# Storing a softmax tile two loads behind instead of three, with the last stores between the last exponentials

## The chip, the cores and the metric

One core of a Trainium2 chip runs the kernel. The metric is the device time of one execution in microseconds; a profiled execution also gives a span, about 1.8 us shorter. Executions of one kernel mostly agree within 0.3%. Differences below are a few microseconds of 1330, so most kernels were timed in five rounds, interleaved with the kernel before on the same chip.

## The reference

```python
# x: float32 [4, 4096, 4352], G = 8 groups of 544 columns in every row
x_g = x.reshape(B, N, G, Dg)
x_g = x_g - x_g.max(axis=-1, keepdims=True)
exp = np.exp(x_g)
out = exp / exp.sum(axis=-1, keepdims=True)
```

Each of the 16384 rows is read once and written once: 285.2 MB in, 285.2 MB out.

## The kernel before

A tile is 128 partitions x 2 rows, 4.46 MB; there are 64 tiles in 6 buffers, worked in place. The sync engine issues the loads, VectorE takes the maxima and scales, ScalarE takes the exponentials and issues the stores.

```python
R = 2; NT = 6; LAG = 3             # rows of a partition, buffers, tiles between load and store
# ... (cut: views, semaphores, take() waits for a semaphore and lowers it)

def vector_max(n):                 # row n: 1 reduction; at a tile's first row wait for its load, raise `seen`
def vector_scale(n):               # row n: wait for its exponentials, 1 reciprocal, 8 multiplications

def scalar_exp(n):
    take(nc.scalar, max_done)
    for g in range(G):
        i = nc.scalar.activation(...)          # exp(x - max), sums accumulated
    i.then_inc(exp_done, 1)

def store(b, target):
    take(nc.scalar, scaled, R)
    nc.scalar.dma_start(out=target, in_=bufs[b][:, :]).then_inc(stored[b], 16)

def scalar_tile(j, target=None):
    take(nc.scalar, seen)
    if target is not None:
        store((j - LAG) % NT, target)
    for r in range(R):
        scalar_exp(j * R + r)

for t in range(nt):                            # the loads' queue
    if t >= NT:
        nc.sync.wait_ge(stored[t % NT], 16 * (t // NT))
    nc.sync.dma_start(out=bufs[t % NT][:, :], in_=xt[t]).then_inc(landed[t % NT], 16)

for j in range(LAG):                           # ScalarE's program
    scalar_tile(j)
with loop(nc.scalar) as u:
    for b in range(NT):
        scalar_tile(LAG + b, turn_out[u, b])
for j in range(rest, nt):
    scalar_tile(j, ot[j - LAG])
for t in range(nt - LAG, nt):
    store(t % NT, ot[t])
# ... (cut: VectorE's program: maximum of row n+1, then scaling of row n; a loop of 12 rows)
```

Of the kernel before, what the change touches and what calls it, by code (L numbers as in the profile page):

```python
# [1 line left out]

# [5 lines left out]


@with_exitstack  # L10
def kernel(
    ctx: ExitStack,
    tc: tile.TileContext,
    x: bass.AP,
    out: bass.AP,
):
    nc = tc.nc
    G = 8
    P = 128
    R = 2  # L20
    NT = 6
    S = R * NT
    LAG = 3
    xf = x.flatten_outer_dims()
    of = out.flatten_outer_dims()
    N, D = xf.shape
    Dg = D // G
    nt = N // (P * R)
    turns = (nt - LAG) // NT
    rest = LAG + turns * NT  # L30
    f32 = mybir.dt.float32
    X = mybir.AxisListType.X
    Exp = mybir.ActivationFunctionType.Exp
    xt = xf.rearrange("(t p r) d -> t p (r d)", p=P, r=R)
    ot = of.rearrange("(t p r) d -> t p (r d)", p=P, r=R)
    turn_out = of[:turns * S * P, :].rearrange("(u b p r) d -> u b p (r d)", b=NT, p=P, r=R)

    landed = [tc.alloc_semaphore(f"landed{b}") for b in range(NT)]
    stored = [tc.alloc_semaphore(f"stored{b}") for b in range(NT)]
    seen = tc.alloc_semaphore("seen")  # L40
    max_done = tc.alloc_semaphore("max_done")
    exp_done = tc.alloc_semaphore("exp_done")
    rec_done = tc.alloc_semaphore("rec_done")
    scaled = tc.alloc_semaphore("scaled")

    ctx.enter_context(tc.tile_critical(no_gpsimd_drain=True))  # L46
    bufs = [ctx.enter_context(nc.sbuf_tensor(f"xt{b}", [P, R * D], f32)) for b in range(NT)]
    mx = ctx.enter_context(nc.sbuf_tensor("mx", [P, S, G], f32))
    sm = ctx.enter_context(nc.sbuf_tensor("sm", [P, S, G], f32))
    rs = ctx.enter_context(nc.sbuf_tensor("rs", [P, S, G], f32))  # L50

    def loop(engine):

        return nc.Fori(
            0, turns, engines=OrderedEngineSet([engine.engine]), head_slot={engine.engine: 0})

    def take(engine, sem, n=1):
        engine.sem_inc(sem, -n).wait_op(sem, n, "sem-ge")  # L58

    def row(s):  # L60
        b, r = divmod(s, R)
        return bufs[b][:, r * D:(r + 1) * D].rearrange("p (g d) -> p g d", g=G)

    def vector_max(n):
        s = n % S
        if s % R == 0:
            take(nc.vector, landed[s // R], 16)
            nc.vector.sem_inc(seen, 1)
        nc.vector.reduce_max(out=mx[:, s, :], in_=row(s), axis=X, negate=True).then_inc(max_done, 1)  # L69

    def vector_scale(n):
        s = n % S
        take(nc.vector, exp_done)
        nc.vector.reciprocal(out=rs[:, s, :], in_=sm[:, s, :]).then_inc(rec_done, 1)  # L74
        take(nc.vector, rec_done)
        xr = row(s)
        for g in range(G):
            i = nc.vector.tensor_scalar_mul(  # L78
                out=xr[:, g, :], in0=xr[:, g, :], scalar1=rs[:, s, g:g + 1])
        i.then_inc(scaled, 1)  # L80

    def scalar_exp(n):
        s = n % S
        take(nc.scalar, max_done)
        xr = row(s)
        for g in range(G):
            i = nc.scalar.activation(  # L87
                out=xr[:, g, :],
                in_=xr[:, g, :],
                func=Exp,  # L90
                bias=mx[:, s, g:g + 1],
                scale=1.0,
                accum_out=sm[:, s, g:g + 1],
            )
        i.then_inc(exp_done, 1)

    def store(b, target):
        take(nc.scalar, scaled, R)
        nc.scalar.dma_start(out=target, in_=bufs[b][:, :]).then_inc(stored[b], 16)

    def scalar_tile(j, target=None):

        take(nc.scalar, seen)
        if target is not None:
            store((j - LAG) % NT, target)
        for r in range(R):
            scalar_exp(j * R + r)


    for t in range(nt):  # L110
        b = t % NT
        if t >= NT:
            nc.sync.wait_ge(stored[b], 16 * (t // NT))
        nc.sync.dma_start(out=bufs[b][:, :], in_=xt[t]).then_inc(landed[b], 16)
    for b in range(NT):
        nc.sync.wait_ge(stored[b], 16 * ((nt - b + NT - 1) // NT))


    nc.scalar.preload_act_table(Exp)  # L119
    for j in range(LAG):  # L120
        scalar_tile(j)
    with loop(nc.scalar) as u:
        for b in range(NT):
            scalar_tile(LAG + b, turn_out[u, b])
    for j in range(rest, nt):
        scalar_tile(j, ot[j - LAG])
    for t in range(nt - LAG, nt):
        store(t % NT, ot[t])


    def vector_rows(lo, hi):
        for n in range(lo, hi):
            vector_max(n + 1)
            vector_scale(n)

    vector_max(0)
    vector_rows(0, LAG * R)
    with loop(nc.vector):
        vector_rows(LAG * R, LAG * R + S)
    vector_rows(rest * R, nt * R - 1)  # L140
    vector_scale(nt * R - 1)


# [1 line left out]
_INS = ['x']  # L145
_OUTS = [((4, 4096, 4352), 'float32')]


# [23 lines left out]
```

## Time and profile before

| | before |
|---|---|
| time, median of the first 3 runs | 1334.18 us |
| span of the profiled run | 1332.2 us |
| share of VectorE, ScalarE | 78%, 57% |
| load, store: median from issue to landing | 28.4, 33.2 us |
| steady rate of the transfers | 433 GB/s |

The first two numbers are the metric and what the profile accounts for. The shares say that no compute engine bounds the kernel; the steady rate says that the transfers do. The two medians show that each transfer spends most of its time queued: a tile alone needs 10.3 us of all 16 engines. The prediction shows the lines.

Two readings below go under the profile's tables, to the trace's record of every DMA packet. A packet is one partition's part of a tile, 34816 bytes in 1.288 us, on one of 16 DMA engines. The records don't name the engine, but an engine's next packet starts 3 ns before its last one ends, so packets can be joined end to end into chains, one for each engine. Near the end of a run the joins are plain; earlier, several engines often end within a few ns of one another, and a long chain is then one of several that fit. *Idleness* of a stretch is its length minus the packet time in it over 16, each packet counted 3 ns shorter for the overlap.

### The profile page before, as it was taken

The page shows a single profiled execution, that of the slowest core. Times are in us where ns is not written, and L with a number is a line of the kernel's source. Part 1 is how long each engine was busy: PE and PEld are TensorE (multiplying, and loading weights), DVE is VectorE, ACT ScalarE, POOL GpSimd, SP SyncE. Part 2 cuts the span into 40 slices and gives each one's busy share as a digit, 9 for nine tenths or more (in the row PEclk, how much of TensorE's full clock was granted, in tenths as well). Part 3 has the DMA queues.
Part 4 walks back from the last instruction along what each step waited for, and adds up shares of the span by engine and source line. Part 5 has one row for each costly group of instructions (what it writes and reads, how often), then busy time and mean ns, then how long its engine had stood idle before and what let it go on. Part 6 is the DMA issues. An engine that isn't in the chain of part 4 may idle for free. (4 is left out here: it accounts for less than half of the span.)

```text
span 1332.2 us, 4328 instructions
## 1 busy us (share of the span) xinstructions
DVE 1041.5 (78%) x1280; ACT 764.4 (57%) x2049; POOL 0.2 (0%) x4
## 2 busy tenths in 40 slices
DVE  5999887877878778778787787877878778778781
ACT  3777655655556555565565655655556555565560
POOL 0000000000000000000000000000000000000000
DMA  9999999999999999999999999999999999999988
GB/s 401 417 400 425 433 431 433 434 433 433 433 432 433 435 435 434 432 433 435 432 433 433 433 433 435 434 434 433 433 434 432 434 433 432 433 435 435 434 373 386
DMA packets 18439, 570.49 MB, mean 428 GB/s; under 512 B 2048, under 2 KB 2048, under 8 KB 2048
## 3 DMA queue, kind: packets, MB, share of 16 engines
q1 hardware_dynamic: 9216, 285.22, 49.7%
q10 hardware_dynamic: 9216, 285.22, 49.7%
q14 instruction: 7, 0.06, 0.0%
HBM read 285.21 MB, written 285.21 MB: 428 GB/s over the span
## 5 line engine op out<-in xcount | busy, mean ns | idle before, releaser
L87 ACT ACTIVATE xt<-xt,mx 128x544 f32<-128x544 f32 x1024 | 751.2, 734 | 536.7 <-ACTq L58 536.7
L69 DVE TENSOR_REDUCE mx<-xt 128x8 f32<-128x4352 f32 x128 | 599.0, 4680 | 240.9 <-DVEq L58 240.9
L78 DVE TENSOR_SCALAR xt<-xt,rs 128x544 f32<-128x544 f32 x1024 | 434.0, 497 | 19.2 <-DVEq L58 0.9
L87 ACT ACTIVATION_READ_ACCUMULATOR xt<-xt,mx 128x1 f32 x1024 | 191.1, 187 | 0.0
L74 DVE RECIPROCAL rs<-sm 128x8 f32<-128x8 f32 x128 | 24.5, 191 | 4.2 <-DVEq L58 4.2
L119 ACT ACT_TABLE_LOAD x1 | 1.3, 1283 | 0.9 <-SPq L46 0.9
L156 POOL MEMSET const-bfloat16-1.0<- 128x1 bf16 x1 | 0.1, 103 | 0.0
L156 POOL MEMSET const-uint8-127<- 128x1 uint8 x1 | 0.1, 102 | 0.0
L156 POOL MEMSET const-float32-0.0<- 128x1 f32 x1 | 0.1, 100 | 0.2 <-issue 0.2
L156 POOL MEMSET const-float32-1.0<- 128x1 f32 x1 | 0.1, 99 | 0.0
## 6 DMA issues: line engine op xcount, KB each, us to landing
xt<-in_x_dram SPq DMA_DIRECT2D x64, 4352.0 KB, 28.4
out_dram<-xt ACTq DMA_DIRECT2D x64, 4352.0 KB, 33.2
```

The lines of the kernel that those rows point to most:

```text
L69: nc.vector.reduce_max(out=mx[:, s, :], in_=row(s), axis=X, negate=True).then_inc(max_done, 1)
L74: nc.vector.reciprocal(out=rs[:, s, :], in_=sm[:, s, :]).then_inc(rec_done, 1)
L78: i = nc.vector.tensor_scalar_mul(out=xr[:, g, :], in0=xr[:, g, :], scalar1=rs[:, s, g:g + 1])
L87: i = nc.scalar.activation(out=xr[:, g, :], in_=xr[:, g, :], func=Exp, bias=mx[:, s, g:g + 1], scale=1.0, accum_out=sm[:, s, g:g + 1],)
L119: nc.scalar.preload_act_table(Exp)
L156: nc = _bacc.Bacc("TRN2", target_bir_lowering=False, num_devices=1)
```

## The change

The intent: start each store one tile earlier, and keep the last stores from waiting behind the last exponentials in ScalarE's program.

```diff
-    LAG = 3
+    LAG = 2
...
-    def scalar_tile(j, target=None):
+    def scalar_tile(j, *targets):
         take(nc.scalar, seen)
-        if target is not None:
-            store((j - LAG) % NT, target)
         for r in range(R):
+            if r < len(targets):
+                store((j - LAG + r) % NT, targets[r])
             scalar_exp(j * R + r)
...
-    for j in range(rest, nt):
-        scalar_tile(j, ot[j - LAG])
-    for t in range(nt - LAG, nt):
-        store(t % NT, ot[t])
+    scalar_tile(nt - 2, ot[nt - 4])
+    scalar_tile(nt - 1, ot[nt - 3], ot[nt - 2])
+    store((nt - 1) % NT, ot[nt - 1])
```

More of the change, by code (lines that the diff above doesn't have):

```diff
@@ L30 @@
     rest = LAG + turns * NT
+    assert rest == nt - 2
     f32 = mybir.dt.float32
```

## The prediction

> **What bounds the kernel now.** I read the first part of the page for the engines, then the row of DMA shares and its rates, then the two queues.
>
> ```profile
> span 1332.2 us, 4328 instructions
> DVE 1041.5 (78%) x1280; ACT 764.4 (57%) x2049; POOL 0.2 (0%) x4
> ...
> DMA  9999999999999999999999999999999999999988
> GB/s 401 417 400 425 433 431 433 434 433 433 433 432 433 435 435 434 432 433 435 432 433 433 433 433 435 434 434 433 433 434 432 434 433 432 433 435 435 434 373 386
> ...
> q1 hardware_dynamic: 9216, 285.22, 49.7%
> q10 hardware_dynamic: 9216, 285.22, 49.7%
> ```
>
> No compute engine is near its limit (VectorE 78%), while the 16 DMA engines are at 90% or more in all but the last two slices. The loads' queue (q1) and the stores' queue (q10) carry the same bytes and take 49.7% each, 99.4% together. The rate is flat at 433 GB/s from the fifth slice on; it sags only in the first four slices and the last two. So the transfers bound the kernel, and a change that moves no byte can only win back what those edges lose: 570.4 MB at the steady 433.2 GB/s (the packet records between 300 and 1200 us) would take 1316.8 us, so **15.4 us of the span is all there is to win**, and part of that is start-up and shutdown.
>
> The second view is the waits of the loads' queue, the third is a table by stretch at both edges (columns: stretch, VectorE busy, ScalarE busy, GpSimd, granted clock, DMA share, GB/s).
>
> ```profile
> SPq L114 <- DMA out_dram<-xt: 1230.8, 58, 74.5
> ...
> 60.00:70.00 10.00, 9.85 (x15) 7.67 (x22) 0.00 (x0) 1.00 0.80 339
> 70.00:80.00 10.00, 9.85 (x11) 7.72 (x23) 0.00 (x0) 1.00 0.97 415
> ...
> 600.00:620.00 20.00, 16.28 (x20) 11.93 (x32) 0.00 (x0) 1.00 1.01 437
> ...
> 1280.00:1290.00 10.00, 6.88 (x8) 3.51 (x11) 0.00 (x0) 1.00 0.92 393
> 1290.00:1300.00 10.00, 9.40 (x14) 7.71 (x22) 0.00 (x0) 1.00 0.67 286
> 1300.00:1310.00 10.00, 3.59 (x9) 1.99 (x6) 0.00 (x0) 1.00 0.92 397
> ```
>
> The first line shows that each of the 58 loads after the first six waits for a store to free its buffer. The rest show two holes in the transfers: one near 66 us, a larger one near 1296 us. The timeline of the end says why the larger one is there (start, length, engine, line, operation).
>
> ```profile
> 1282.97 4.69 DVE L69 TENSOR_REDUCE mx<-xt 128x8 f32<-128x4352 f32 x1 [4.12 <-DVEq L58]
> 1283.07 0.35 ACTq L99 DMA_DIRECT2D out_dram<-xt  x1
> ...
> 1297.69 0.35 ACTq L99 DMA_DIRECT2D out_dram<-xt  x1
> 1298.16 0.37 ACTq L99 DMA_DIRECT2D out_dram<-xt  x1
> ...
> 1305.98 0.34 ACTq L99 DMA_DIRECT2D out_dram<-xt  x1
> ```
>
> The last load landed at 1282.7. Store 60 is issued at once, but stores 61 and 62, whose data is ready (tile 61 long before, tile 62 when the scaling begun at 1287.92 ends at about 1291.3), sit in ScalarE's program behind both rows of the last tile's exponentials. From store 60's last packet to store 61's first there is nothing to move.
>
> **What the Trainium skill says.** "DMA: Bandwidth & Descriptors", section Issuing engines are not separate DMA queues: transfers from different issuing engines run on the same 16 engines and interleave. The trace agrees: loads and stores hold half the busy time each. The same page, section Queues, rings and completion order, says each engine serves its queues in turn, packet by packet. It agrees too: in steady stretches q1 moves 216 of 433 GB/s. Its section Where 436 GB/s comes from puts the fabric's ceiling at 435.2 GB/s; the trace's steady 433.2 is at it, so deeper queues can't raise the plateau. Its section Anatomy of one DMA gives some 2 us of fixed cost per transfer; here the first packet comes about 1 us after a store's issue and a load's landing record about 1.7 us after its last packet (1280.96 to 1282.7). That cost shows only where a queue has run dry.
>
> **The change part by part.** No work is added or removed: 64 loads, 64 stores, 1024 exponentials as before; only the place of the stores in ScalarE's order moves.
>
> *Steady part.* A buffer's round is 6 tiles times the load-to-load period of 20.67 us (landing records), 124.0 us. Now it is 28.4 (load) + 62.5 (landed to store issued: three periods and 0.5) + 33.1 (store). With a lag of two the middle is 41.8, so load and store together must fill 82.2 instead of 61.5. Both queues already always hold work: load t is issued (1233.6 for tile 62) before load t-1 lands (1241.4), and stores overlap likewise. So the extra 20.7 us is only queueing, and the period stays 20.67: **0 us**. Is the data ready? VectorE's order is maximum of row n+1, then scaling of row n; when tile j is seen, tile j-2 was scaled two row-slots (8.3 us each) earlier. No new wait.
>
> *Head.* Store 0 is issued at 60.6, with tile 3. There VectorE, at 16.5 us a tile (two rows of 4.68 + 0.19 + 3.39), lags the loads, which arrive every 10.3. One tile earlier is 44.1. The first store's issue lasts 5.4 us (the others 0.34), and its first packet came 5.9 us after its start, so packets begin near 50. The loads still have 15 us of work then (load 5's last packet is near 65), so the two share: store 0 needs 20.6, ends near 70.6, and load 5 near 80. Load 6 is issued near 72 instead of 78.4 and queues behind load 5; store 1 is queued from 60. The hole between 60 and 80 is closed: adding the DMA idleness of the packet records, 1.25 (60 to 66), 0.53 (66 to 70), 0.46 (70 to 80) and 0.09 gives **2.3 us** saved. Carrying this bookkeeping on, stores run further behind: I expect about 30.5 us from load issue to landing and 51.5 for a store, the sum 82.
>
> *Tail.* When load 63 lands (call it T) store 59, issued two periods earlier, would by the 51.5 us need 10 more at half rate, so about 4.8 us of unshared work, store 60 is queued and store 61 is issued within 0.5 us: packets until T+25 (4.8 + two times 10.3). Store 62 needs tile 62 scaled, before at T+8.6, and is issued near T+9, far ahead of T+25; it covers until T+36. Store 63 stays at T+23.3 (1305.98 minus 1282.7). No hole is left, and the end is at about T+46. Before, idleness between 1280 and the last packet at 1330.02 was 50.0 minus 45.05 busy, 5.0, of which 0.3 is the finish: **4.6 us** saved on the average engine.
>
> *Sum.* On the average DMA engine 2.3 + 4.6 = 6.9 us, so 1327.3. But joining each engine's packets end to end shows one engine behind the others in the tail: its packets run without a break from 1277 to 1330.02, while the other fifteen idle about 4.2 us before store 61. It has no tail hole to lose, only the head's 2.6 us (1.75 + 0.55 + 0.3). If that lag comes back, the time falls only to 1334.2 - 2.6 = 1331.6. I choose nearly between: **1330.0 us**.
>
> **The rivals.** (1) *The late engine takes the place of the hole*: the fifteen others finish early and wait. For it: its unbroken packets above. Against: its lag may be chance of this execution. Time 1331.6. (2) *All holes close for all engines*: 1327 to 1328. (3) *ScalarE stalls*, because the store of tile 62 holds its queue until the scaling ends and delays the last exponentials, hence store 63. Against: that scaling ends at 1291.3 and the last row's exponentials begin at 1296.03, and store 63 has 10 us in hand; time unchanged. (4) *Hidden anyway*: stores start earlier, but the loads slow by as much and nothing is regained in the head; with the tail bound by the late engine, 1334. (5) *The deeper queue shifts the steady rate*: mixed and single-direction packets both take 1.29 us, so I see no cause.
>
> **Range and chances.** From all holes closed plus a little luck (slow packets near 81, 96 and 178 us cost over 2 us and may not return) to nearly nothing: 1326.3 to 1333.0. Two per cent is 26.7 us, more than the whole 15.4 us that a perfect stream could regain; a loss of that size needs the steady rate to break. Faster 0.01, same 0.98, slower 0.01.
>
> **What would show it.** Right: first store issued near 44, load 6 near 72; medians to landing near 30.5 and 51.5; the 60 to 70 and 1290 to 1300 stretches at 430 GB/s; stores 61 and 62 issued at T+0.5 and T+9; period still 20.67. Wrong: a stretch under 430 GB/s in the middle, a hole before store 62 or 63, a longer wait of ScalarE at the end, or closed holes with the last packets of one engine trailing by several microseconds (rival 1 in full).

## The result

The changed kernel takes 1330.23 us (median of 4 runs, 1330.04 to 1333.27), the kernel before 1334.12 (4 runs). The ratio is 0.9976, 95% interval 0.9959 to 0.9993: about 3.9 us faster, and "the same" at 2%. A ratio here is the mean time of one kernel's runs over that of the other's of the same rounds, so it is not quite the ratio of the medians. Of the changed kernel's runs one was 3 us slower, which pulls the mean; five more (run e0) gave 1330.25, 1330.19 to 1331.29.

From the page of the changed kernel:

```profile
span 1328.5 us, 4328 instructions
...
DMA  9999999999999999999999999999999999999997
GB/s 403 418 436 435 434 433 429 432 435 436 435 433 428 432 435 436 435 434 430 429 436 435 435 434 433 426 436 436 434 434 433 427 435 436 435 434 433 427 433 328
...
xt<-in_x_dram SPq DMA_DIRECT2D x64, 4352.0 KB, 30.5
out_dram<-xt ACTq DMA_DIRECT2D x64, 4352.0 KB, 51.3
```

The sag of the third slice (400 before) and of the last but one (373 before) is gone; the last slice is worse than before, 328 for 386. Stores take 51.3 us to land instead of 33.2, which is queueing, since the middle rate is unchanged. Its table by stretch (VectorE busy, ScalarE busy, GpSimd, clock, DMA share, GB/s):

```profile
60.00:70.00 10.00, 9.70 (x14) 6.70 (x19) 0.00 (x0) 1.00 1.03 443
...
1290.00:1300.00 10.00, 7.18 (x11) 7.27 (x20) 0.00 (x0) 1.00 1.03 446
1300.00:1310.00 10.00, 3.40 (x8) 0.00 (x0) 0.00 (x0) 1.00 1.02 442
1310.00:1320.00 10.00, 0.00 (x0) 0.00 (x0) 0.00 (x0) 1.00 0.93 404
1320.00:1328.00 8.00, 0.00 (x0) 0.00 (x0) 0.00 (x0) 1.00 0.06 26
```

Both holes are closed: the stretch from 1290 to 1300 has a share of 1.03 where it had 0.67. The last line is the new thing. From 1320 on the share is 0.06, one sixteenth, and the rate 26 GB/s, what one DMA engine moves (433 / 16 is 27). The chains say the same: thirteen engines are done by 1320.4, two end at 1322.45 and one, alone, at 1326.31. The kernel ends with **one late DMA engine**; I call it that from here on.

Before, the late engine can't be seen in such a table, since the hole in the tail let it catch up: fifteen engines idled 4 us before store 61 while it went on. All ended together, at 1329.6 to 1330.02.

The timeline of the end, for the stores' places:

```profile
1280.54 4.69 DVE L70 TENSOR_REDUCE mx<-xt 128x8 f32<-128x4352 f32 x1 [4.08 <-DVEq L59]
1280.63 0.35 ACTq L100 DMA_DIRECT2D out_dram<-xt  x1
...
1288.98 0.34 ACTq L100 DMA_DIRECT2D out_dram<-xt  x1
...
1303.55 0.34 ACTq L100 DMA_DIRECT2D out_dram<-xt  x1
```

The last load lands at 1280.3. Stores 61, 62 and 63 follow it by 0.3, 8.7 and 23.3 us; store 62 went out between the last tile's two rows.

### The profile page after: what moved, and what is told of

Same layout as the page of the kernel before. It is cut to its first block, busy times and chain, and to the rows that moved or that the text cites. A ratio compares the mean times of both kernels' runs of the same rounds, so it can differ in the third digit from the quotient of the medians.

```text
span 1328.5 us, 4328 instructions
## 1 busy us (share of the span) xinstructions
DVE 1041.7 (78%) x1280; ACT 764.5 (58%) x2049; POOL 0.2 (0%) x4
## 6 DMA issues: line engine op xcount, KB each, us to landing
xt<-in_x_dram SPq DMA_DIRECT2D x64, 4352.0 KB, 30.5
out_dram<-xt ACTq DMA_DIRECT2D x64, 4352.0 KB, 51.3
```

## The experiments

**Theory.** The late DMA engine sets the end. It never had the hole in the tail, so closing that hole gains nothing; the gain is the hole in the head, where all 16 engines ran dry. **Rivals.** The average engine counts, and the tail gave most of it; or the deeper queue of stores during the whole run did. A second question is what makes an engine late.

| run | what is different | time, us (runs) | idleness 40 to 100 us | idleness 1276 to 1319 us | last packet |
|---|---|---|---|---|---|
| before | | 1334.1 to 1334.3 (9 each) | 2.28 | 4.63 | 1330.02 |
| after | lag 2, last stores early | 1330.23 (4) | 0 | 0 | 1326.31 |
| e0 | after again | 1330.25 (5) | | | 1326.40 |
| e1 | lag 2 alone | 1329.97 (5) | 0 | 0 | 1326.53 |
| e2 | lag 3, last stores early | 1333.96 (5) | 2.20 | 0.14 | 1330.02 |
| e4 | lag 2, store 0 as late as before | 1330.18 (5) | 0 | 0 | 1326.26 |
| e8 | lag 2, stores 0 and 1 later still | 1337.56 (5) | 7.14 | 0 | 1333.52 |
| e9 | lag 3, stores 0 and 1 together | 1331.00 (5) | 0 | 4.22 | 1326.06 |

**e0, the changed kernel again.**

> The changed kernel again, on the same chip as the three runs beside it, for its spread. Every theory: 1330.0 to 1330.5 us, with a run or two 3 us longer as before. If one late DMA engine sets the end, the profile shows its last packets trailing the others' by 5 us or more, in a last stretch of a few us at about 1/16 of the rate.

1330.25 us, ratio 0.9972 (0.9958 to 0.9985). It is in the range named; one run of five was 1 us longer. The late engine is there again (last packet 1326.40, most others 1320.5).

**e1, the lag alone.**

```diff
-    scalar_tile(nt - 1, ot[nt - 3], ot[nt - 2])
+    scalar_tile(nt - 1, ot[nt - 3])
+    store((nt - 2) % NT, ot[nt - 2])
     store((nt - 1) % NT, ot[nt - 1])
```

> The lag of two alone; stores 62 and 63 after all exponentials of the last tile. By my bookkeeping store 62 is then issued 15 us after the last load lands instead of 9, and the earlier stores keep the engines supplied until 25 us after it, so: 1330.2 us, no difference to the changed kernel above 0.5 us. Rival, that the interleaving of the last stores brought the gain: 1333 or more.

1329.97 us, ratio 0.9968 (0.9954 to 0.9982). The second half of the change, the stores between the exponentials, does nothing that can be measured once the lag is two: the stores already queued keep the engines supplied (idleness 0).

**e2, the early last stores alone.**

```diff
# against the kernel before, after the loop
+    take(nc.scalar, seen)
+    store((nt - 4) % NT, ot[nt - 4])
+    store((nt - 3) % NT, ot[nt - 3])
+    scalar_exp((nt - 1) * R)
+    store((nt - 2) % NT, ot[nt - 2])
+    scalar_exp((nt - 1) * R + 1)
+    store((nt - 1) % NT, ot[nt - 1])
```

> The lag of three kept; only the last stores go out early (60 and 61 when the last tile is seen, 62 between its rows). Both theories: the hole between 1294 and 1299 us closes. Theory one, a late DMA engine that had no hole there sets the end: 1333.4 to 1334.2 us, as before within 0.8. Theory two, the average engine sets it: 4.6 us less, about 1329.5.

1333.96 us, ratio 0.9997 (0.9983 to 1.0011): nothing. Its table by stretch:

```profile
1290.00:1300.00 10.00, 8.11 (x11) 7.72 (x23) 0.00 (x0) 1.00 1.02 440
...
1320.00:1330.00 10.00, 0.00 (x0) 0.00 (x0) 0.00 (x0) 1.00 0.42 181
```

The hole is gone, and fifteen engines end by 1324.7 instead of 1329.7. The late one ends at 1330.02, to the hundredth where it did before. A hole of 4.6 us that shows plainly in the profile was worth nothing, because the one engine that sets the end had work all through it. This settles the first rival.

**e4, the first store held at its old place.**

```diff
# against e1
-    for j in range(LAG):
+    for j in range(HEAD - 1):           # HEAD = 4
         scalar_tile(j)
+    take(nc.scalar, seen)
+    store(0, ot[0])
+    store(1, ot[1])
+    for r in range(R):
+        scalar_exp((HEAD - 1) * R + r)
     with loop(nc.scalar) as u:          # from tile 4 on; nothing left after it but the last two stores
```

> Lag of two throughout as in e1, but store 0 is held back to the place that it had before (with tile 3), with store 1 right behind it; same amount of code. If the gain comes from the early first store, which keeps the engines fed while the first six loads run out, the hole near 66 us comes back and the late engine loses about 2 us again: 1332 to 1334 us. Rival, the gain comes from the deeper queue of stores during the whole run: 1330.0 us as in e1.

1330.18 us. **A miss, and it does not tell the two apart**, since the hole that it was to bring back did not come (idleness 0). The timelines say why. First the kernel before, then e4:

```profile
60.55 5.44 ACTq L99 DMA_DIRECT2D out_dram<-xt  x1
```

```profile
63.10 0.39 ACTq L101 DMA_DIRECT2D out_dram<-xt  x1
63.61 2.57 ACTq L101 DMA_DIRECT2D out_dram<-xt  x1
```

Before, the first store is the first DMA inside ScalarE's loop and its issue lasts 5.4 us; in e4 it stands ahead of the loop and takes 0.39. Its packets begin at 64.45 instead of 66.49, just before the first six loads are through, and store 1 is right behind. So the place of the first store alone did not make the hole before: a slow first issue and a second store that came 16 us after the first went with it. What makes an issue slow is not known (store 1 in e4, also ahead of the loop, took 2.57 us); e3 and e7 below bear on it.

**e8, a real hole in the head.** As e4, with the two stores one row later.

```diff
     take(nc.scalar, seen)
+    scalar_exp((HEAD - 1) * R)
     store(0, ot[0])
     store(1, ot[1])
-    for r in range(R):
-        scalar_exp((HEAD - 1) * R + r)
+    scalar_exp((HEAD - 1) * R + 1)
```

> As e4 (lag of two), but stores 0 and 1 are held back further, to between the two rows of tile 3: some 7 us later, after the first six loads have run out. If a hole in the head costs every DMA engine, the late one too, and so the end: a hole of 5 to 7 us and 1335 to 1337.5 us. Rival, what counts is the depth of the stores' queue in the steady part, as deep here as in e4: 1330.2.

1337.56 us, ratio 1.0026 (1.0012 to 1.0039):

```profile
60.00:70.00 10.00, 9.70 (x14) 6.60 (x17) 0.00 (x0) 1.00 0.41 175
70.00:80.00 10.00, 9.85 (x15) 7.72 (x23) 0.00 (x0) 1.00 0.91 390
```

The idleness is 7.14 us, and the last packet comes 7.2 us after that of the changed kernel, although the steady queue of stores is as deep (median 53.6 us to landing). A hole in the head costs its full length, as all engines have it.

**e9, no hole in the head, but the old lag.** Against the kernel before: nothing is stored with tile 4, the loop starts at tile 5.

```diff
+    take(nc.scalar, seen)               # tile 3
+    store(0, ot[0])
+    store(1, ot[1])
+    for r in range(R):
+        scalar_exp(LAG * R + r)
+    scalar_tile(LAG + 1)                # tile 4, no store
     with loop(nc.scalar, aturns) as u:
         for b in range(NT):
-            scalar_tile(LAG + b, turn_out[u, b])
+            scalar_tile(HEAD + b, turn_out[u, b])
```

> The steady lag of three of the kernel before and its late last stores, but in the head stores 0 and 1 go out together with tile 3, so that nothing runs dry there. If the head's holes were the whole gain: no hole near 66 us, 1330 to 1331 us, although the tail keeps its hole and the steady queue its old depth (median store 33 to 36 us to landing). Rival, the deeper queue of the lag of two brings the gain: 1333.5 to 1334.5.

1331.00 us, ratio 0.9977 (0.9963 to 0.999): nearly the whole gain, with the lag of three, a median store of 33.2 us as before, and the hole in the tail still there:

```profile
60.00:70.00 10.00, 9.85 (x16) 7.66 (x21) 0.00 (x0) 1.00 1.00 391
70.00:80.00 10.00, 9.85 (x11) 7.72 (x23) 0.00 (x0) 1.00 1.01 436
...
1290.00:1300.00 10.00, 7.12 (x15) 5.96 (x16) 0.00 (x0) 1.00 0.68 289
```

This settles the second rival: the depth of the queue in the steady part is worth the remaining 0.8 us at most, which is within the scatter. (Its first line has share 1.00 but 391 GB/s: some packets there take longer than 1.288 us.)

**What makes an engine late? e3, e6, e7: more instructions, the same work.** The profile lists a third queue, q14, that carries the program's own instructions, 8192 bytes at a time. In e3 the loops of ScalarE and VectorE are unrolled, in e6 VectorE's alone, in e7 ScalarE's alone.

```diff
-    with loop(nc.scalar) as u:                     # e3, e7
-        for b in range(NT):
-            scalar_tile(LAG + b, turn_out[u, b])
+    for j in range(LAG, rest):
+        scalar_tile(j, ot[j - LAG])
...
-    with loop(nc.vector):                          # e3, e6
-        vector_rows(LAG * R, LAG * R + S)
-    vector_rows(rest * R, nt * R - 1)
+    vector_rows(LAG * R, nt * R - 1)
```

> The changed kernel with ScalarE's and VectorE's loops unrolled: the same transfers and arithmetic, some 25 more instruction fetches of 8 KB on queue 14. Theory, the fetches fall on one or two of the 16 DMA engines and make those late: at about 0.6 us each on 12 or 13 more per engine, 1336 to 1340 us, with the last stretch at a small share of the rate longer by as much. Rival, the fetches are spread over all engines or cost nothing: 1330 to 1331.5 us.

> The changed kernel with VectorE's loop alone unrolled: some 16 more instruction fetches. In e3 the two kinds of fetch seemed to differ in cost (0.6 and 0.95 us) and engine. If VectorE's fetches fall on the second-latest DMA engine, which ends 3.9 us before the latest: 16 times 0.6 is 9.9 us, less 3.9: 1334 to 1337 us. If they fall on the latest engine: 1339 to 1341. If spread over many: 1330 to 1331.5.

> The changed kernel with ScalarE's loop alone unrolled: some 10 more instruction fetches. If they fall on the latest DMA engine at 0.95 us each: 1338 to 1340 us. If spread over many engines: 1330 to 1331.5.

1339.67, 1340.70 and 1340.74 us; e3's ratio is 1.0036 (1.0023 to 1.005). The changed kernel's line of that queue, then e3's, with e3's last stretch:

```profile
q14 instruction: 7, 0.06, 0.0%
```

```profile
q14 instruction: 32, 0.26, 0.0%
...
1330.00:1340.00 10.00, 0.00 (x0) 0.00 (x0) 0.00 (x0) 1.00 0.05 22
```

With twenty-five fetches more, 0.2 MB beside 570 MB and 0.0% of the DMA time, the kernel was 9.4 us slower: the last packet came at 1336.33 instead of 1326.31. In the packet records each fetch takes 0.31 us and the packet behind it on the same engine is mostly 0.2 to 0.65 us longer, together 0.7 on average: about 0.9 for VectorE's, 0.6 for ScalarE's. Spread over 16 engines that would be about 1 us. But followed back from the last packet of e3, the chain of the latest engine can be joined through the fetches of 1264.79, 1158.78 and 1053.13, VectorE's, about every 105 us.

e6 agrees: 10 more fetches, VectorE's, the one of 1265.60 on the chain that ends last, and the last packet 10.8 us later (1337.15). I had expected 16 of VectorE and 10 of ScalarE; it is 10 and 15. That both together (e3) cost no more than VectorE's alone fits two kinds on two engines, of which the later counts. e7 is less clean: its runs scatter from 1337.15 to 1347.09, and the transfers have a hole before 1300 (share 0.33), because its last load lands at 1297.8 instead of 1280.3; why is open. So it shows that unrolling ScalarE costs too, but neither through which engine nor that the fetches do it.

The fetches are not all of it in e3 and e6 either. From about 1010 us on in e3, 1030 in e6 and 1185 in e7, many packets on several engines take up to 1.3 us too long, mostly with no fetch before them. Between 200 and 1270 us, packets longer than 1.288 us cost 3.7, 3.2 and 3.0 us per engine, against 0.36 in the changed kernel, and less than 0.8 of that lies right behind a fetch. So that unrolling costs 9 to 11 us is shown; how much of it the fetches do is not.

The Trainium skill, "Runtime: NRT & Kernel Launch", section Instruction fetch mechanics, has the sequencer fetch its next block with its own DMA queue and calls the cost of a block boundary "mostly hidden". These runs differ: whatever the sequencer sees of it, in a kernel bound by the DMA engines a fetch is also paid on one of them, at 0.6 to 0.9 us. The same section says that a branch out of the window forces a fetch; the 5.4 us of the first issue in the loop, with fetches at 63.5 and 64.2 us in that very time, look like that. But in e3 and e7 ScalarE has no loop, and the first store's issue is still slow, 4.42 and 3.42 us (e3's line):

```profile
43.66 4.42 ACTq L100 DMA_DIRECT2D out_dram<-xt  x1
```

So the loop's branch is not the whole cause of the slow issue, which stays open.

**In the changed kernel itself the late engine is late for another reason.** From 660 to 800 us, with no fetch near, one chain of 108 packets has 0.67 us of extra, spread over some 40 packets that are 5 to 32 ns too long, mostly stores (35 of 42); the other fifteen have 0.00. From 200 to 1240 us, where no fetch occurs at all, such packets add up to 5.4 us, and in each stretch of 40 us about nine tenths of it can be put on a single chain (a quarter, where the same lengths are strewn over the stores at random). If it is one engine throughout, that is nearly all by which the late engine trails the thirteen (6.1 us). And it is not the engine of the fetches: before 1000 us in e3, e6 and e7, the chain that holds these packets runs past the fetches without one on it (the time of e6 lies in the range named for the latest engine, but not for that reason). So e3, e6 and e7 show a second way to make an engine late, not the one at work here. All kernels' records hold the slightly long packets. What they are is **open**.

**e5, taking work off the late engine by another cut.**

```diff
-    store((nt - 1) % NT, ot[nt - 1])
+    take(nc.scalar, scaled, R)
+    for lo, hi in ((0, 120), (120, 128)):
+        nc.scalar.dma_start(out=ot[nt - 1][lo:hi, :], in_=bufs[b][lo:hi, :]).then_inc(stored[b], 16)
```

> The changed kernel, with the last store cut in two: 120 partitions (15 DMA engines, 8 rows each) and the last 8 partitions (8 engines, one row each). If the late engine is the one left out, it loses 8 packets of 1.29 us and the end is set by the others: 1326 to 1327.5 us. If it is one of the 8 that get a row more: 1331.5. If neither: 1330.2.

1340.39 us: **a failed attempt**, worse than any case that I had named. Its table by stretch:

```profile
1310.00:1320.00 10.00, 0.00 (x0) 0.00 (x0) 0.00 (x0) 1.00 1.00 299
1320.00:1330.00 10.00, 0.00 (x0) 0.00 (x0) 0.00 (x0) 1.00 0.56 157
```

The engines are as busy, but at 299 GB/s: of the 122 packets that start after 1310.6, 64 take over 1.35 us, 19 of them 2.71 and two over 5.1, instead of 1.29. The Trainium skill, "DMA: Bandwidth & Descriptors", section Why a DMA increments its semaphore by 16 and not by 1, has the rule for how many engines a shape gets, by which it is 15 for 120 partitions and 8 for 8; one engine does end at 1310.6, without packets of the last store, and it isn't the late one. Why the packets are slow is open. Cutting a transfer away from 128 partitions was no way to rebalance.

**e10, fewer instructions.** The eight multiplications of a row become one, with the reciprocals broadcast.

```diff
-        for g in range(G):
-            i = nc.vector.tensor_scalar_mul(
-                out=xr[:, g, :], in0=xr[:, g, :], scalar1=rs[:, s, g:g + 1])
-        i.then_inc(scaled, 1)
+        wide = rs[:, s, :].rearrange("p (g o) -> p g o", o=1).broadcast_to([P, G, Dg])
+        nc.vector.tensor_mul(xr, xr, wide).then_inc(scaled, 1)
```

> The changed kernel with VectorE's eight multiplications of a row made one (the reciprocals broadcast), which about halves VectorE's instructions. If its instruction fetches make the latest DMA engine late (0.95 us each, three of them before), one or two fewer give 1328 to 1329.5 us, as long as the longer multiplication (estimate 4.5 us a row for 3.4, so some 19 us a tile, under the 20.66 of the transfers) keeps up. If it doesn't keep up or opens a hole in the head: over 1331.

1329.74 us (1329.71 to 1329.82), ratio 0.9965 (0.9952 to 0.9979). The direction is right, the size is short of the range: only one fetch fewer (6), last packet 1325.77 instead of 1326.31. That the missing fetch is the cause is not shown: the changed kernel and its near copies (e0, e1, e4) scatter from 1326.26 to 1326.53 themselves, and their late engine is not late by fetches. VectorE does more for it, 4.69 us for a row's scaling instead of 3.39, and is 91% busy, still under the transfers. It is the fastest version here, by half a microsecond, and also the one with the least room.

## Why the prediction was right

*The bound* was read rightly. Nothing in the steady part moved: load to load it is 20.66 us (20.67 before).

*Steady part, 0 us:* right, and the medians to landing came out at 30.5 and 51.3 us for 30.5 and 51.5. e9 shows that the deeper queue is worth little by itself (0.8 us at most).

*Head, 2.3 us:* the mechanism was right, the times in it were not. Store 0 was issued at 48.6, not 44.1, its first packet came at 58, not 50, and load 6 at 77.5, not 72; the issue alone took 5.4 us again. The loop's entry seems to be what delayed it: in e3 and e7, which have no loop on ScalarE, store 0 is issued at 43.7 and 43.4. The hole closed all the same. e8 and e9 make it causal. It was under-sized: the late engine gained 3.7 us (1330.02 to 1326.31), of which its idleness accounts for 2.6 (1.75 + 0.55 + 0.3, as the prediction added). Packets slower than 1.288 us between 20 and 200 us cost 2.7 us per engine before and 1.0 after. That is 1.7 us, and with it the sum is close; the prediction had named these packets as luck and put them only into the range. Whether the change makes them fewer is not shown; they vary, 1.5 in e0 (the same kernel), 2.2 in e2, 1.3 in e4, 1.6 in e1. These are means over all engines, not the late engine's own.

*Tail, 4.6 us on the average engine:* the hole closed exactly as laid out (stores 61 and 62 at 0.3 and 8.7 us after the last load, end 46.0 us after it), and it gained nothing, as e2 shows. This is the step to learn from: the sum of 6.9 us on the average engine was the wrong sum.

*The choice "nearly between":* rival 1, the late engine in full, was what happened, and the prediction had listed just this among the signs that it was wrong. 1330.0 was hit by luck, because two errors cancelled: the tail's 4.6 us did not count, and the head was worth more than its 2.6. Rival 1 alone had said 1331.6. Rival 2 (1327 to 1328) is refuted by e2, rival 3 (ScalarE stalls) by store 63 leaving at 23.3 us as before, rival 4 (hidden anyway) by the result, rival 5 by the unchanged rate.

## What to carry to other kernels

In a stream bound by transfers, ask of each hole in the profile whether *all* DMA engines have it: a hole at the start costs its full length, a hole near the end may only be the time in which a late engine catches up. Keep the second direction of traffic ready before the first runs dry; two stores queued together at the right time did as much as a shorter lag throughout. And count instructions even where no engine is busy: every fetch is a transfer on some one of the engines that bound the kernel, 0.6 to 0.9 us of its time here, and unrolling a loop cost 9 to 11 us.

## What the Trainium skill lacked or had wrong

- "Runtime: NRT & Kernel Launch", Instruction fetch mechanics: the cost of fetching is called mostly hidden, and full unrolling preferred. Here a fetch of 8192 bytes cost a DMA engine about 0.7 us, and the kernel with both loops unrolled (25 more) was 9.4 us of 1330 slower.
- No page that I read says that these fetches fall unevenly on the DMA engines: with 10 more of VectorE's the last packet came 10.8 us later, one of them on the chain that ended last.
- "DMA: Bandwidth & Descriptors", Why a DMA increments its semaphore by 16 and not by 1: it gives the number of engines for 120 partitions, but not the speed. As 120 and 8 partitions, 19 of the last packets took 2.71 us and two over 5.1 instead of 1.29, and the kernel 10 us longer.
- No page that I read has a time for the slow first store: its issue took 5.4 us in the loop, 4.42 and 3.42 with the loop unrolled, against 0.34 to 0.39 for nearly all others.
- "DMA: Bandwidth & Descriptors", Latency and other measured facts, has engines 7 and 15 as usually slower and ties it to transfers issued from GpSimd. Here none are, and still one engine's packets, mostly stores, ran some 0.5% long (0.67 us in 140); the records don't name the engine, and the cause is open.
